# A gated product on 8192 x 8192 floats: four-row groups packed into three 64 KiB slots, with all transfers issued from one software queue

## The chip, the cores and the metric

The kernel runs on one core of a Trainium2 chip. Times are device microseconds (us). Most executions of one kernel agree within 0.3%. Every experiment below was therefore timed in five rounds beside the kernel before (nine runs of it in each batch; r0_after has four timed runs, the others five). All runs were fast, with a granted clock of 1.0.

A ratio is the mean time of one kernel's fast runs over that of the kernel before in the same rounds, so it is not quite the ratio of the medians that are quoted beside it. Brackets after it are its 95% interval.

## The reference

```python
def reference(x):                       # x: 8192 x 8192 float32
    a, b = np.split(x, 2, axis=-1)
    return a * (1 / (1 + np.exp(-b)))   # 8192 x 4096 float32
```

268.4 MB are read and 134.2 MB written. Each element needs one sigmoid (ACT, the scalar engine) and one product (DVE, the vector engine).

## The kernel before

The default path takes two rows per partition (PAIR = 2). Loads are issued from the SP queue, stores from the ACT queue.

```python
x_t   = x.rearrange("(n p r) m -> n p (r m)", p=P, r=PAIR)     # 32 tiles, 64 KiB per partition
out_t = out.rearrange("(n p r) m -> n p (r m)", p=P, r=PAIR)
for i in range(n_tiles):
    x_sb = pool.tile([P, in_cols], fp32)        # two buffers of 64 KiB
    o_sb = pool.tile([P, out_cols], fp32)       # two buffers of 32 KiB
    eng(LOAD_ENG, i).dma_start(out=x_sb, in_=x_t[i])            # SP
    n_chunks = TAIL_CHUNKS if i >= n_tiles - TAIL_ITERS else 1  # last tile in 4 chunks a row
    for r in range(PAIR):
        # ... a_part, b_part, o_part: slices of the row, n_chunks of them
        nc.scalar.activation(out=b_part, in_=b_part, func=SIG)
        nc.vector.tensor_mul(out=o_part, in0=a_part, in1=b_part)
        # ... in the last tile: store o_part at once (512 KB)
    if n_chunks == 1:
        eng(STORE_ENG, i + 1).dma_start(out=out_t[i], in_=o_sb) # ACT, 4 MiB
```

Of the kernel before, what the change touches and what calls it, by code (L numbers as in the profile page):

```python
# [2 lines left out]

# [4 lines left out]


@with_exitstack  # L10
def kernel(
    ctx: ExitStack,
    tc: tile.TileContext,
    x: bass.AP,
    out: bass.AP,
):
    nc = tc.nc
    P = nc.NUM_PARTITIONS

    PAIR = int(os.environ.get("GLU_PAIR", "2"))  # L20
    BUFS = int(os.environ.get("GLU_BUFS", "2" if PAIR == 2 else "5"))
    STORE_ENG = os.environ.get("GLU_STORE", "scalar")
    LOAD_ENG = os.environ.get("GLU_LOAD", "sync")
    TAIL_CHUNKS = int(os.environ.get("GLU_TAIL_CHUNKS", "4"))
    TAIL_ITERS = int(os.environ.get("GLU_TAIL_ITERS", "1"))

    n_rows, n_cols = x.shape
    half = n_cols // 2
    assert out.shape == (n_rows, half)

    fp32 = mybir.dt.float32
    SIG = mybir.ActivationFunctionType.Sigmoid

    def eng(name, i):
        if name == "alt":
            name = "sync" if (i % 2 == 0) else "scalar"
        return getattr(nc, name)

    pool = ctx.enter_context(tc.tile_pool(name="io", bufs=BUFS))

    if PAIR == 1:
        x_t = x.rearrange("(n p) m -> n p m", p=P)
        out_t = out.rearrange("(n p) m -> n p m", p=P)
        n_tiles = x_t.shape[0]

        for i in range(n_tiles):
            x_sb = pool.tile([P, n_cols], fp32)
            eng(LOAD_ENG, i).dma_start(out=x_sb, in_=x_t[i])

            n_chunks = TAIL_CHUNKS if i >= n_tiles - TAIL_ITERS else 1  # L50
            csz = half // n_chunks
            for c in range(n_chunks):
                lo = c * csz
                hi = lo + csz
                a_part = x_sb[:, lo:hi]
                b_part = x_sb[:, half + lo : half + hi]
                nc.scalar.activation(out=b_part, in_=b_part, func=SIG)
                nc.vector.tensor_mul(out=a_part, in0=a_part, in1=b_part)
                eng(STORE_ENG, i + 1).dma_start(out=out_t[i, :, lo:hi], in_=a_part)
    else:  # L60
        x_t = x.rearrange("(n p r) m -> n p (r m)", p=P, r=PAIR)
        out_t = out.rearrange("(n p r) m -> n p (r m)", p=P, r=PAIR)
        n_tiles = x_t.shape[0]
        in_cols = PAIR * n_cols
        out_cols = PAIR * half

        for i in range(n_tiles):
            x_sb = pool.tile([P, in_cols], fp32)
            o_sb = pool.tile([P, out_cols], fp32)
            eng(LOAD_ENG, i).dma_start(out=x_sb, in_=x_t[i])  # L70

            n_chunks = TAIL_CHUNKS if i >= n_tiles - TAIL_ITERS else 1
            for r in range(PAIR):
                a_all = x_sb[:, r * n_cols : r * n_cols + half]
                b_all = x_sb[:, r * n_cols + half : (r + 1) * n_cols]
                o_all = o_sb[:, r * half : (r + 1) * half]
                csz = half // n_chunks
                for c in range(n_chunks):
                    lo = c * csz
                    hi = lo + csz  # L80
                    a_part = a_all[:, lo:hi]
                    b_part = b_all[:, lo:hi]
                    o_part = o_all[:, lo:hi]
                    nc.scalar.activation(out=b_part, in_=b_part, func=SIG)  # L84
                    nc.vector.tensor_mul(out=o_part, in0=a_part, in1=b_part)  # L85
                    if n_chunks > 1:
                        eng(STORE_ENG, i + 1).dma_start(  # L87
                            out=out_t[i, :, r * half + lo : r * half + hi], in_=o_part
                        )
            if n_chunks == 1:  # L90
                eng(STORE_ENG, i + 1).dma_start(out=out_t[i], in_=o_sb)


# [1 line left out]
_INS = ['x']  # L95
_OUTS = [((8192, 4096), 'float32')]


# [23 lines left out]
```

## Time and profile before

The median was 937.13 us (936.40 to 937.37, three runs). The first fence holds lines of the profile page of the kernel before: busy time of each engine, DVE's and the DMA engines' busy tenths in 40 slices, what the DMA engines moved in each slice, the two DMA queues (packets, MB, share of the 16 engines' span), and the chain of waits by engine.

```profile
...
DVE 280.9 (30%) x70; ACT 230.0 (25%) x71; POOL 0.2 (0%) x4
...
DVE  0333321333213332133321333312333123331234
...
DMA  9999999999999999999999999999999999999998
GB/s 404 404 449 427 427 449 427 427 434 464 404 441 434 428 449 425 451 408 462 410 429 446 425 450 420 453 408 453 421 429 446 424 452 429 441 411 450 424 449 359
...
q1 hardware_dynamic: 4608, 268.44, 66.5%
q10 hardware_dynamic: 5616, 134.22, 33.3%
...
HBM read 268.44 MB, written 134.22 MB: 431 GB/s over the span
...
DMA 78%; DVE 15%; ACT 6%; issue 0%; DVEq 0%; ACTq 0%; SPq 0%
...
```

The two queues take 66.5% + 33.3% = 99.8% of the 16 DMA engines' time. DVE and ACT are busy for less than a third. DVE is part of the chain (15%) only because a tile's second half of work stands between a landing and the next load; while it runs, the other buffers' transfers are moving.

The trace also holds one record for each packet (one piece of a transfer, moved by one of the 16 engines), which the views above only add up. From these records:

| packet | count | usual time of one | sum / 16 engines |
|---|---|---|---|
| load, 64 KiB | 4096 | 2418 ns | 619 us |
| store, 32 KiB | 3968 | 1213 ns | 301 us |
| store of the last tile, 4 KiB | 1024 | 159 ns | 10 us |

The sum is 930 us of a span of 934.1. 65,536 bytes in 2418 ns on 16 engines are 433.7 GB/s. The Trainium skill (DMA: Bandwidth & Descriptors, Where 436 GB/s comes from) puts the ceiling of the 16 ports at 435.2 GB/s; the trace agrees. So no rearrangement can gain much more than the 4 us that are not packets.

The next fence is the timeline of the kernel before near its end: start, length, engine, line, operation, and in brackets the idle time before it with what ended it.

```profile
...
885.91 7.12 ACT L84 ACTIVATE x_sb<-x_sb 128x4096 f32<-128x4096 f32 x2 [21.92 <-DMA x_sb<-in_x_dram]
889.56 8.76 DVE L85 TENSOR_TENSOR o_sb<-x_sb 128x4096 f32<-128x4096 f32 x2 [20.28 <-ACT x_sb L84]
898.35 0.34 ACTq L91 DMA_DIRECT2D out_dram<-o_sb  x1
914.83 2.95 ACT L84 ACTIVATE x_sb<-x_sb 128x1024 f32<-128x1024 f32 x3 [21.79 <-DMA x_sb<-in_x_dram]
...
```

A tile's work starts every 28.9 us (885.91, 914.83). That is close to eight rounds of one load packet and one store packet, 8 x (2418 + 1213) = 29,048 ns: the two queues alternate, nearly packet by packet.

### The profile page before, as it was taken

The page shows a single profiled execution, that of the slowest core. Times are in us where ns is not written, and L with a number is a line of the kernel's source. Part 1 is how long each engine was busy: PE and PEld are TensorE (multiplying, and loading weights), DVE is VectorE, ACT ScalarE, POOL GpSimd, SP SyncE. Part 2 cuts the span into 40 slices and gives each one's busy share as a digit, 9 for nine tenths or more (in the row PEclk, how much of TensorE's full clock was granted, in tenths as well). Part 3 has the DMA queues.
Part 4 walks back from the last instruction along what each step waited for, and adds up shares of the span by engine and source line. Part 5 has one row for each costly group of instructions (what it writes and reads, how often), then busy time and mean ns, then how long its engine had stood idle before and what let it go on. Part 6 is the DMA issues. An engine that isn't in the chain of part 4 may idle for free.

```text
span 934.1 us, 410 instructions
## 1 busy us (share of the span) xinstructions
DVE 280.9 (30%) x70; ACT 230.0 (25%) x71; POOL 0.2 (0%) x4
## 2 busy tenths in 40 slices
DVE  0333321333213332133321333312333123331234
ACT  0313331133311333113332033320233202333023
POOL 0000000000000000000000000000000000000000
DMA  9999999999999999999999999999999999999998
GB/s 404 404 449 427 427 449 427 427 434 464 404 441 434 428 449 425 451 408 462 410 429 446 425 450 420 453 408 453 421 429 446 424 452 429 441 411 450 424 449 359
DMA packets 10226, 402.67 MB, mean 431 GB/s; under 512 B 1136, under 2 KB 1136, under 8 KB 2160
## 3 DMA queue, kind: packets, MB, share of 16 engines
q1 hardware_dynamic: 4608, 268.44, 66.5%
q10 hardware_dynamic: 5616, 134.22, 33.3%
q14 instruction: 2, 0.02, 0.0%
HBM read 268.44 MB, written 134.22 MB: 431 GB/s over the span
## 4 chain that ended last, share of the span: by engine, by line
DMA 78%; DVE 15%; ACT 6%; issue 0%; DVEq 0%; ACTq 0%; SPq 0%
DMA x_sb<-in_x_dram 78%; DVE o_sb L85 15%; ACT x_sb L84 6%; DVEq L117 0%; ACTq L87 0%; SPq L70 0%; ACTq L84 0%
## 5 line engine op out<-in xcount | busy, mean ns | idle before, releaser
L85 DVE TENSOR_TENSOR o_sb<-x_sb 128x4096 f32<-128x4096 f32 (+1 forms) x70 | 280.9, 4056 | 647.3 <-ACT x_sb L84 647.3
L84 ACT ACTIVATE x_sb<-x_sb 128x4096 f32<-128x4096 f32 (+1 forms) x70 | 228.7, 3315 | 696.1 <-DMA x_sb<-in_x_dram 692.0
L84 ACT ACT_TABLE_LOAD x1 | 1.3, 1283 | 0.7 <-PEq L106 0.7
L106 POOL MEMSET const-bfloat16-1.0<- 128x1 bf16 x1 | 0.1, 102 | 0.0
L106 POOL MEMSET const-uint8-127<- 128x1 uint8 x1 | 0.1, 102 | 0.0
L106 POOL MEMSET const-float32-1.0<- 128x1 f32 x1 | 0.1, 99 | 0.0
L106 POOL MEMSET const-float32-0.0<- 128x1 f32 x1 | 0.1, 98 | 0.2 <-issue 0.2
## 6 DMA issues: line engine op xcount, KB each, us to landing
out_dram<-o_sb ACTq DMA_DIRECT2D x31, 4096.0 KB, 41.8
out_dram<-o_sb ACTq DMA_DIRECT2D x8, 512.0 KB, 6.3
x_sb<-in_x_dram SPq DMA_DIRECT2D x32, 45.5
```

The lines of the kernel that those rows point to most:

```text
L84: nc.scalar.activation(out=b_part, in_=b_part, func=SIG)
L85: nc.vector.tensor_mul(out=o_part, in0=a_part, in1=b_part)
L106: nc = _bacc.Bacc("TRN2", target_bir_lowering=False, num_devices=1)
```

## The change

The intent, as the code shows it: 64 KiB runs in both directions, all transfers 8 MiB, no output buffers (results are packed into the slot whose inputs are already used up), and one queue whose fixed order decides which transfer comes next. The tail order (last second-half load before the last store but one) is there so that the last compute runs under a store.

```diff
-    pool = ctx.enter_context(tc.tile_pool(name="io", bufs=BUFS))
... (the old loop, shown above, goes)
+    R = 4
+    n_groups = n_rows // (P * R)
+    x_g = x.rearrange("(n p h r) m -> n h p (r m)", p=P, h=2, r=R // 2)
+    out_g = out.rearrange("(n p r) m -> n p (r m)", p=P, r=R)
+    width = 2 * n_cols
+    pool = ctx.enter_context(tc.tile_pool(name="slots", bufs=1))
+    heads = [pool.tile([P, width], fp32, name=f"head{k}") for k in range(2)]
+    tail = pool.tile([P, width], fp32, name="tail")
+    def load(g, h):
+        nc.gpsimd.dma_start(out=heads[g % 2] if h == 0 else tail, in_=x_g[g, h])
+    def compute(g):
+        head = heads[g % 2]
+        for r in range(R):
+            src = head if r < 2 else tail
+            lo = (r % 2) * n_cols
+            a = src[:, lo : lo + half]
+            b = src[:, lo + half : lo + n_cols]
+            nc.scalar.activation(out=b, in_=b, func=SIG)
+            nc.vector.tensor_mul(out=head[:, r * half : (r + 1) * half], in0=a, in1=b)
+    def store(g):
+        nc.gpsimd.dma_start(out=out_g[g], in_=heads[g % 2])
+    load(0, 0)
+    load(0, 1)
+    for g in range(n_groups):
+        last_pair = g >= n_groups - 2
+        if g + 1 < n_groups:
+            load(g + 1, 0)
+        compute(g)
+        if g + 1 < n_groups and last_pair:
+            load(g + 1, 1)
+        store(g)
+        if g + 1 < n_groups and not last_pair:
+            load(g + 1, 1)
```

The queue thus carries: load, load, load, store 0, load, load, store 1, and so on, with the last two stores side by side.

More of the change, by code (lines that the diff above doesn't have):

```diff
@@ L1 @@
-import os
 from contextlib import ExitStack
@@ L5 @@
 import concourse.tile as tile
-from concourse import bass_utils, mybir
+from concourse import mybir
 from concourse._compat import with_exitstack
@@ L18 @@
     P = nc.NUM_PARTITIONS
-    PAIR = int(os.environ.get("GLU_PAIR", "2"))
-    BUFS = int(os.environ.get("GLU_BUFS", "2" if PAIR == 2 else "5"))
-    STORE_ENG = os.environ.get("GLU_STORE", "scalar")
-    LOAD_ENG = os.environ.get("GLU_LOAD", "sync")
-    TAIL_CHUNKS = int(os.environ.get("GLU_TAIL_CHUNKS", "4"))
-    TAIL_ITERS = int(os.environ.get("GLU_TAIL_ITERS", "1"))
+    fp32 = mybir.dt.float32
+    SIG = mybir.ActivationFunctionType.Sigmoid
     n_rows, n_cols = x.shape
     half = n_cols // 2
-    assert out.shape == (n_rows, half)
@@ L31 @@
-    fp32 = mybir.dt.float32
-    SIG = mybir.ActivationFunctionType.Sigmoid
-    def eng(name, i):
-        if name == "alt":
-            name = "sync" if (i % 2 == 0) else "scalar"
-        return getattr(nc, name)
-    pool = ctx.enter_context(tc.tile_pool(name="io", bufs=BUFS))
-    if PAIR == 1:
-        x_t = x.rearrange("(n p) m -> n p m", p=P)
-        out_t = out.rearrange("(n p) m -> n p m", p=P)
-        n_tiles = x_t.shape[0]
-        for i in range(n_tiles):
-            x_sb = pool.tile([P, n_cols], fp32)
-            eng(LOAD_ENG, i).dma_start(out=x_sb, in_=x_t[i])
-            n_chunks = TAIL_CHUNKS if i >= n_tiles - TAIL_ITERS else 1
-            csz = half // n_chunks
-            for c in range(n_chunks):
-                lo = c * csz
-                hi = lo + csz
-                a_part = x_sb[:, lo:hi]
-                b_part = x_sb[:, half + lo : half + hi]
-                nc.scalar.activation(out=b_part, in_=b_part, func=SIG)
-                nc.vector.tensor_mul(out=a_part, in0=a_part, in1=b_part)
-                eng(STORE_ENG, i + 1).dma_start(out=out_t[i, :, lo:hi], in_=a_part)
-    else:
-        x_t = x.rearrange("(n p r) m -> n p (r m)", p=P, r=PAIR)
-        out_t = out.rearrange("(n p r) m -> n p (r m)", p=P, r=PAIR)
-        n_tiles = x_t.shape[0]
-        in_cols = PAIR * n_cols
-        out_cols = PAIR * half
-        for i in range(n_tiles):
-            x_sb = pool.tile([P, in_cols], fp32)
-            o_sb = pool.tile([P, out_cols], fp32)
-            eng(LOAD_ENG, i).dma_start(out=x_sb, in_=x_t[i])
-            n_chunks = TAIL_CHUNKS if i >= n_tiles - TAIL_ITERS else 1
-            for r in range(PAIR):
-                a_all = x_sb[:, r * n_cols : r * n_cols + half]
-                b_all = x_sb[:, r * n_cols + half : (r + 1) * n_cols]
-                o_all = o_sb[:, r * half : (r + 1) * half]
-                csz = half // n_chunks
-                for c in range(n_chunks):
-                    lo = c * csz
-                    hi = lo + csz
-                    a_part = a_all[:, lo:hi]
-                    b_part = b_all[:, lo:hi]
-                    o_part = o_all[:, lo:hi]
-                    nc.scalar.activation(out=b_part, in_=b_part, func=SIG)
-                    nc.vector.tensor_mul(out=o_part, in0=a_part, in1=b_part)
-                    if n_chunks > 1:
-                        eng(STORE_ENG, i + 1).dma_start(
-                            out=out_t[i, :, r * half + lo : r * half + hi], in_=o_part
-                        )
-            if n_chunks == 1:
-                eng(STORE_ENG, i + 1).dma_start(out=out_t[i], in_=o_sb)
```

## The prediction

> **What bounds it now.** The DMA engines. The page's slice table shows DMA at 9 tenths in 39 of 40 slices, mean 431 GB/s; DVE is busy 30%, ACT 25%. The queue table adds up to 99.8% (66.5% loads, 33.3% stores). In the trace's transfer records nearly every 64 KiB load packet takes 2418 ns and every 32 KiB store packet 1213 ns, alone or mixed with the other direction: about 433 GB/s on 16 engines, whatever the mix. Floor: 4096 load packets / 16 x 2.418 + 3968 store packets / 16 x 1.213 + 1024 small store packets / 16 x 0.159 = 619 + 301 + 10 = 930 us of a 934.1 us span. Only some 4 us are anything else: about 2 us before the first packet, under 1 us of slow first packets, a 1 us hiccup at the first store, and about 2 us at the end, where the 512 KB stores leave engines partly idle (windows view: DMA share 0.69 in the last 6 us). The chain of waits names loads (78%), DVE (15%) and ACT (6%), but its compute hides behind other transfers.
>
> **What the change does.** Bytes stay at 402.65 MB. Stores become 64 KiB runs: 2048 packets at an estimated 2.418 us for 3968 of 1.213 and 1024 of 0.159: about 1.5 us saved. 71 transfers become 48 of 8 MiB. Loads and stores follow each other in one queue instead of alternating by packet; with equal rates both ways that alone changes nothing.
>
> **Does the queue run dry?** From the trace: 8 MiB takes 8 x 2.418 = 19.3 us. A store needs its group's second half landed plus 3.6 (ACT) + 2 x 4.39 (DVE) = 12.4 us; meanwhile the next group's first half moves (19.3 us), which leaves 7 us to issue. The load that needs a store's completion waits while a second-half load (19.3 us) moves. At the end the last second half is loaded before the last store but one, so the last 12.4 us of compute hide too. No bubble; the final store runs at full rate: 1 to 2 us saved.
>
> **What it adds.** GpSimd writes descriptors in software. The Trainium skill (DMA: Bandwidth & Descriptors, Latency and other measured facts) gives a first byte of about 1 us against 0.6: only the first load exposes it. It also warns (SBUF — State Buffer, "DVE blocks DMA" box) that DVE 2-port operations starve this path; here issues come after the multiplies or with 7 to 19 us of slack. No run shows either yet.
>
> **Sum.** 934.1 - 1.5 (packets) - 1.5 (tail) + 0.5 (first issue) + up to 3 (direction switches in one queue) = 932 to 935 span; measured time lies 3 us above the span. I predict 936 us, range 930 to 948. Faster by over 2%: 0.01; within 2%: 0.94; slower by over 2%: 0.05.
>
> **What would show it.** One software queue, DMA at 9 throughout, about 432 GB/s; 64 KiB packets of 2.42 us both ways; each issue several us before the preceding transfer ends; unchanged ACT and DVE means (3.6, 4.4 us); no drop of DMA share in the tail.
>
> **What would make it wrong.** Descriptors cut small (4 KiB packets take 159 ns here, 5% slower per byte); one slow engine, which a serial queue cannot hide; a 1 us stall at each of the 29 direction switches, as at the first store here (3%); the 128 KiB pitch of the loads slowing HBM; descriptor generation held up by DVE beyond 7 us.

## The result

The changed kernel took 942.70 us median (940.58 to 942.86, four runs) against 936.92 (four runs): ratio 1.0059 [1.0045, 1.0073]. It is slower by 0.6%, inside the predicted range, but on the other side of the old time than the sum in the prediction. In a later batch on one chip it took 944.11 (ratio 1.0081 [1.0067, 1.0095]). The result is correct.

These are the lines of the page after that answer to those before; the last three are groups of GpSimd's DMA instructions (busy time, mean ns of one, idle before, what ended most of it).

```profile
...
DVE 281.8 (30%) x64; ACT 229.2 (24%) x65; POOL 25.7 (3%) x52
...
DVE  0452330513305133051331503315033250332430
...
DMA  9999999999999999999999999999999999999997
GB/s 401 432 415 443 404 446 446 426 421 446 426 421 443 446 415 432 446 426 432 435 440 429 429 437 435 429 432 432 443 424 432 440 443 412 437 443 412 437 415 315
...
q0 software_dynamic: 6912, 402.66, 99.2%
...
HBM read 268.44 MB, written 134.22 MB: 428 GB/s over the span
...
issue 79%; DMA 14%; POOL 2%; DVE 1%; ACT 0%; POOLq 0%; PEldq 0%; ACTq 0%
...
L53 POOL DMA_DIRECT2D out_dram<-head x16 | 8.6, 536 | 496.6 <-DVE head L50 496.6
L40 POOL DMA_DIRECT2D head<-in_x_dram x16 | 8.6, 536 | 358.8 <-DMA out_dram<-head 358.0
L40 POOL DMA_DIRECT2D tail<-in_x_dram x16 | 8.4, 527 | 31.6 <-DVE head L50 31.3
...
```

DVE and ACT do the same work in the same time. One software queue carries all. DMA stays at 9 until the last slice, where it is 7 and moves 315 GB/s, before 359. GpSimd needs 527 to 536 ns for one issue. The chain of waits is of no use for this kernel: 79% of it is "issue", time in which the profile shows nothing that the engine waited for.

The windows view shows the end more closely. Columns: window, its length, busy time of DVE, ACT and POOL with instruction counts, clock, DMA share, GB/s. First the kernel before, where the DMA share drops at 930:

```profile
...
core 0: us, DVE busy (x) ACT busy (x) POOL busy (x), PEclk, DMA share, GB/s
...
700.00:800.00 100.00, 26.28 (x6) 22.53 (x7) 0.00 (x0) 1.00 1.01 436
...
925.00:930.00 5.00, 2.36 (x2) 1.83 (x2) 0.00 (x0) 1.00 1.03 420
930.00:935.00 5.00, 0.00 (x0) 0.00 (x0) 0.00 (x0) 1.00 0.41 169
935.00:942.00 7.00, 0.00 (x0) 0.00 (x0) 0.00 (x0) 1.00 0.00 0
...
```

Then the changed kernel, with the same windows:

```profile
...
700.00:800.00 100.00, 26.46 (x6) 21.37 (x6) 2.11 (x4) 1.00 1.00 433
...
925.00:930.00 5.00, 0.00 (x0) 0.00 (x0) 0.00 (x0) 1.00 1.00 433
930.00:935.00 5.00, 0.00 (x0) 0.00 (x0) 0.00 (x0) 1.00 0.64 275
935.00:942.00 7.00, 0.00 (x0) 0.00 (x0) 0.00 (x0) 1.00 0.02 9
...
```

In the middle (700 to 800) nothing is lost: share 1.00 and 433 GB/s. Three things are to be seen at the end. There is a drop after 930 here too. It is slow: a share of 0.64 for 5 us means that some engines are done and others are not; 0.02 of 7 us on 16 engines is 2.2 us, about one packet of one engine. And the span ends at 941 us, some 3 us after that last packet.

The packet records give the whole account, in us. "Slow" is what packets took beyond 2418, 1213 or 159 ns, averaged over the 16 engines; "last engine" is how much later the last engine ends than the mean of all; "after" is the time from the last byte to the end. In these tables the end, and with it the span, is the start of the last instruction, 0.05 us before the end of the span on the page. The columns add up to some 1 to 1.5 us more than the span, because successive packets' records overlap by 3 to 4 ns; the kernel before has more packets, so the differences add up to 6.2 and not to 6.8.

| | first packet starts | packets, usual length | slow | last engine | after | span |
|---|---|---|---|---|---|---|
| before | 1.73 | 930.0 | 1.81 | 0.7 | 1.30 | 934.1 |
| after | 2.65 | 928.5 | 4.91 | 2.7 | 3.02 | 940.9 |
| difference | +0.9 | -1.5 | +3.1 | +2.0 | +1.7 | +6.8 |

Three of these differences need no argument. The packets became fewer and cheaper, as foreseen (-1.5). The first packet starts 1.38 us after GpSimd's issue begins, before 1.00 us after SP's; the Trainium skill's difference of 0.4 us (1 against 0.6, DMA: Bandwidth & Descriptors, Latency and other measured facts) agrees, and another 0.54 us pass because GpSimd begins its first issue at 1.27 us and SP at 0.73. At the end, GpSimd has a DRAIN instruction on record that ends 2.0 us after SP has seen the last store land; in the kernel before, GpSimd's drain at the end is over long before.

The slow packets are not spread out; they gather where one transfer follows another. The records do not name the engine, but joining each to the one that ends where it starts gives 16 chains. In the changed kernel 167 packets after the first 70 us are over 30 ns slow. Of these 114 are the last packet of a load that is followed by a store (2.1 of 3.2 us), 27 stand at a change from a store to a load (0.4 us; that load had been issued some 20 us before, 815.86 for packets that start from 833.6 on), and 15 are the first packet of the very last load (0.4 us). At the first store, all 16 engines are slow, by 0.8 to 1.2 us; at the second 13 by up to 0.35 us; later between 3 and 15 by up to 1 us. The kernel before has one such place, also at its first store, and then practically none (0.10 us from 70 us on, against 3.30). The engines that are hit fall behind: at the end, 11 of the 16 finish within 0.4 us of each other, the other five 1.4 to 3.4 us after the median.

### The profile page after: what moved, and what is told of

The parts are those of the page before. It is cut to its first block, busy times and chain, and to the rows that moved or that the text cites. A ratio compares the mean times of both kernels' runs of the same rounds, so it can differ in the third digit from the quotient of the medians.

```text
span 941.0 us, 315 instructions
## 1 busy us (share of the span) xinstructions
DVE 281.8 (30%) x64; ACT 229.2 (24%) x65; POOL 25.7 (3%) x52
## 4 chain that ended last, share of the span: by engine, by line
issue 79%; DMA 14%; POOL 2%; DVE 1%; ACT 0%; POOLq 0%; PEldq 0%; ACTq 0%
DMA head<-in_x_dram 6%; DMA tail<-in_x_dram 5%; DMA out_dram<-head 3%; DVE head L50 1%; POOL out_dram L53 1%; POOL head L40 1%; POOL tail L40 1%; ACT tail L49 0%; POOLq L92 0%; POOLq L53 0%; POOLq L40 0%; PEldq L92 0%; ACTq L49 0%
## 5 line engine op out<-in xcount | busy, mean ns | idle before, releaser
L50 DVE TENSOR_TENSOR head<-tail 128x4096 f32<-128x4096 f32 x32 | 140.2, 4422 | 438.1 <-ACT tail L49 438.1
L49 ACT ACTIVATE tail<-tail 128x4096 f32<-128x4096 f32 x32 | 114.0, 3608 | 467.4 <-DMA tail<-in_x_dram 467.4
L50 DVE TENSOR_TENSOR head<-head 128x4096 f32<-128x4096 f32 x32 | 141.6, 4425 | 192.2 <-ACT head L49 190.5
L49 ACT ACTIVATE head<-head 128x4096 f32<-128x4096 f32 x32 | 114.0, 3608 | 209.4 <-DMA head<-in_x_dram 209.4
L53 POOL DMA_DIRECT2D out_dram<-head x16 | 8.6, 536 | 496.6 <-DVE head L50 496.6
L40 POOL DMA_DIRECT2D head<-in_x_dram x16 | 8.6, 536 | 358.8 <-DMA out_dram<-head 358.0
L40 POOL DMA_DIRECT2D tail<-in_x_dram x16 | 8.4, 527 | 31.6 <-DVE head L50 31.3
```

The source lines that it names most:

```text
L40: nc.gpsimd.dma_start(out=heads[g % 2] if h == 0 else tail, in_=x_g[g, h])
L49: nc.scalar.activation(out=b, in_=b, func=SIG)
L50: nc.vector.tensor_mul(out=head[:, r * half : (r + 1) * half], in0=a, in1=b)
L53: nc.gpsimd.dma_start(out=out_g[g], in_=heads[g % 2])
```

## The experiments

Candidate explanations for the slow packets and the lagging engines were:

- A: the software path (descriptors written by GpSimd) makes packets slow.
- B: one serial queue that alternates loads and stores makes them slow at each load-to-store switch.
- C: the successor of the slow packet was issued too late.

The table holds all twelve experiments in the columns of the table above (one profiled execution each), with medians and ratios of five rounds. The first four ran on one chip, so did the next four and the last four, on three different chips. Kernels are best compared by their ratios to the kernel before: the changed kernel itself took 942.70 us in one batch and 944.11 in another.

| run | us, median | ratio to before | first | packets | slow | last engine | after | span |
|---|---|---|---|---|---|---|---|---|
| r0_after | 944.11 | 1.0081 [1.0067, 1.0095] | 2.64 | 928.5 | 7.34 | 3.0 | 3.02 | 944.0 |
| e1_sp | 939.75 | 1.0035 [1.0023, 1.0048] | 1.74 | 928.5 | 4.85 | 2.5 | 1.13 | 937.8 |
| e2_two | 981.09 | 1.0477 [1.0455, 1.0499] | 1.72 | 928.5 | 26.50 | 0.1 | 1.12 | 977.0 |
| e3_last_sp | 943.43 | 1.0067 [1.0054, 1.0081] | 2.62 | 928.5 | 6.26 | 2.7 | 1.16 | 940.4 |
| e4_short | 938.24 | 1.0018 [1.0004, 1.0032] | 1.73 | 928.5 | 3.19 | 2.1 | 1.23 | 935.7 |
| d1_sp | 938.42 | 1.0022 [1.0009, 1.0034] | 1.72 | 928.5 | 3.26 | 2.8 | 1.19 | 936.6 |
| b1_loads_pool | 937.41 | 1.0008 [0.9996, 1.0021] | 2.60 | 930.0 | 2.16 | 0.9 | 1.23 | 935.7 |
| b2_stores_pool | 937.41 | 1.0010 [0.9997, 1.0022] | 1.75 | 930.0 | 1.97 | 0.5 | 2.82 | 935.5 |
| d2_pool | 943.62 | 1.0073 [1.0059, 1.0087] | 2.62 | 928.5 | 4.51 | 4.8 | 2.99 | 942.4 |
| d3_grouped | 934.12 | 0.9974 [0.9961, 0.9986] | 1.74 | 928.5 | 1.53 | 0.4 | 1.10 | 932.3 |
| d4_half | 941.12 | 1.0048 [1.0035, 1.0060] | 1.73 | 929.5 | 3.15 | 5.0 | 1.10 | 939.1 |
| e5_pool_short | 941.30 | 1.0049 [1.0037, 1.0062] | 2.64 | 928.5 | 3.27 | 2.4 | 3.08 | 938.9 |

The kernel before had medians of 936.95, 936.66 and 936.71 us.

### r0_after: the changed kernel again

> The changed kernel again, as the yardstick of this call. Every theory expects 941 to 943 us, ratio to the kernel before about 1.006, a software queue, slow packets (over 2418 ns) mostly at the last load packet before each store, and the last engine finishing some 3 us after the first.

It took 944.11 us, above the expected range by 1 us. The extra time is in the slow packets (7.34 us against 4.91 in the first profile); first packet and end are alike to 0.01 us. The slow packets are thus the part that differed most between these two executions; whether by run or by chip is not known. Their places differ too: of 221, some 90 are the last packet of a load before a store and some 80 stand at a change from a store to a load, where together they cost 1.6 us. The kernel is not edited.

### e1_sp: every transfer from the SP queue

```diff
-        nc.gpsimd.dma_start(out=heads[g % 2] if h == 0 else tail, in_=x_g[g, h])
+        nc.sync.dma_start(out=heads[g % 2] if h == 0 else tail, in_=x_g[g, h])
-        nc.gpsimd.dma_start(out=out_g[g], in_=heads[g % 2])
+        nc.sync.dma_start(out=out_g[g], in_=heads[g % 2])
```

> The changed kernel with every transfer issued from the SP queue instead of GpSimd; order, slots, waits and bytes are the same. Theory A (the software path costs the 5.8 us: 0.9 us later first packet, 2 us GpSimd drain at the end, and 3 to 5 us of slow packets and engine skew): 935 to 937 us, no slow packets but the first few. Theory B (the single serial queue makes the slow packets and the skew at each direction switch, the software path only the first packet and the drain): 939 to 940.5 us, slow packets still at each load-to-store switch.

939.75 us, as B has it: 4.4 us less than with GpSimd, and still 2.8 us more than the kernel before. Of the 4.4, the first packet gives 0.9 and the end 1.9; the slow packets stay (170 packets over 30 ns slow after the first 70 us, 167 and 221 in the two profiles with GpSimd). 132 of the 170 are the last packet of a load before a store, and those at a change from a store to a load, 16, cost 0.2 us. Theory A alone falls: slow packets and lagging engines are there without any software descriptor.

### e2_two: the new slots with loads on SP and stores on ACT

```diff
-        nc.gpsimd.dma_start(out=heads[g % 2] if h == 0 else tail, in_=x_g[g, h])
+        nc.sync.dma_start(out=heads[g % 2] if h == 0 else tail, in_=x_g[g, h])
-        nc.gpsimd.dma_start(out=out_g[g], in_=heads[g % 2])
+        nc.scalar.dma_start(out=out_g[g], in_=heads[g % 2])
```

> The changed kernel with loads from the SP queue and stores from the ACT queue, same three slots. If alternating queues only share the engines, as the trace of before shows, a store and the second-half load beside it end together after about 39 us, and the load that waits for that store starts only after it has landed: a bubble of about 2 us in each of 14 groups, 955 to 965 us. If the single queue is itself a cost (theory B) and no bubble arises: 934 to 937 us.

It is slower than both expectations, 981.09 us. Two queues are no improvement in themselves; the three slots need the fixed order. The timeline near the end shows why:

```profile
...
895.88 0.36 ACTq L53 DMA_DIRECT2D out_dram<-head  x1
...
943.02 7.12 ACT L49 ACTIVATE tail<-tail 128x4096 f32<-128x4096 f32 x2 [26.69 <-DMA tail<-in_x_dram]
946.67 8.76 DVE L50 TENSOR_TENSOR head<-tail 128x4096 f32<-128x4096 f32 x2 [24.86 <-ACT tail L49]
955.46 0.34 ACTq L53 DMA_DIRECT2D out_dram<-head  x1
```

The store of group 14 is issued at 895.88 us and shares the engines with the second-half load of group 15, and the load lands at 943 us. Then the last sigmoid and the last product run with almost nothing left to move, and the last store is issued at 955.46. The windows view of the same run (columns as above):

```profile
...
820.00:880.00 60.00, 17.61 (x4) 14.25 (x4) 0.00 (x0) 1.00 0.99 418
...
941.00:957.00 16.00, 8.76 (x2) 7.12 (x2) 0.00 (x0) 1.00 0.15 66
957.00:977.00 20.00, 0.00 (x0) 0.00 (x0) 0.00 (x0) 1.00 0.85 367
...
```

From 941 to 957 the DMA share is 0.15: about 14 us are lost there, which my expectation had left out. Most of the rest are slow packets: 24.7 us of them after the first 70 us, nearly all of them load packets, about 1 to 1.7 us in most groups just before a store joins and mostly 0.4 to 0.9 us around its end. So slow packets come in two queues as well, where the store queue runs empty in each group. The bubbles that I expected between groups come to about 5 us of gaps in the records. So the fixed order in one queue is worth a lot with these slots; it does not follow that it is better than the order before with its own buffers.

### e3_last_sp: only the last store from SP

```diff
-        nc.gpsimd.dma_start(out=out_g[g], in_=heads[g % 2])
+        q = nc.sync if g == n_groups - 1 else nc.gpsimd
+        q.dma_start(out=out_g[g], in_=heads[g % 2])
```

> The changed kernel with only the last store moved to the SP queue. If the 2 us GpSimd drain after the last transfer is charged to software transfers still in flight, it ends earlier and 1.5 to 2 us are saved: 940.5 to 941 us. The last two stores then share the engines packet by packet, which costs nothing. If the drain is charged to the queue as such: 942 to 943 us.

The first theory is the one that says that software transfers still in flight hold the drain up. The end of the span behaves as it says: GpSimd's drain ends at 927 us, under the last store, and the time after the last byte falls from 3.02 to 1.16 us. The total hardly shows it: 943.43 against 944.11, with overlapping intervals and above both expected ranges, so the gain in time is inconclusive; the slow packets, which vary by more than that, were not touched.

### e4_short: on SP, compute cut to 256 columns

The two edits of e1_sp, and this one:

```diff
-            nc.scalar.activation(out=b, in_=b, func=SIG)
-            nc.vector.tensor_mul(out=head[:, r * half : (r + 1) * half], in0=a, in1=b)
+            nc.scalar.activation(out=b[:, :256], in_=b[:, :256], func=SIG)
+            nc.vector.tensor_mul(out=head[:, r * half : r * half + 256], in0=a[:, :256], in1=b[:, :256])
```

> The SP version of the changed kernel (939.75 us) with the sigmoid and the product done on 256 of 4096 columns only; wrong result on purpose. Order, slots, waits and bytes are unchanged, but each store is issued some 18 us before the engines need it, not 5. Theory C (a packet is slow because its successor's descriptors came late): the slow packets before stores vanish, apart from the first few, and 936 to 937 us. Theory B (one serial queue pays at every load-to-store switch): the slow packets stay, 939 to 940 us.

Its output is wrong, which doesn't matter for the time. 938.24 us lies between the theories. Slow packets become fewer (107 after 70 us, from 170) and cost 1.49 us there, from 3.09, but they do not vanish. Theory C is at most a part. The ratio's interval overlaps a little with that of e1_sp, and the cut takes away both the lateness and the work of ACT and DVE beside the transfers, so this run does not tell those two apart.

### d1_sp: transfers alone, same order, on SP

```diff
-    ... (heads, tail, compute and the loop)
+    src = pool.tile([P, width], fp32, name="src")
+    ring = [pool.tile([P, width], fp32, name=f"ring{k}") for k in range(2)]
+    nc.sync.dma_start(out=src, in_=x_g[0, 0])
+    nc.sync.dma_start(out=ring[0], in_=x_g[0, 1])
+    nc.sync.dma_start(out=ring[1], in_=x_g[1, 0])
+    nc.sync.dma_start(out=out_g[0], in_=src)
+    for k in range(3, 2 * n_groups):
+        nc.sync.dma_start(out=ring[(k - 1) % 2], in_=x_g[k // 2, k % 2])
+        if k % 2 == 0:
+            nc.sync.dma_start(out=out_g[k // 2 - 1], in_=src)
+    nc.sync.dma_start(out=out_g[n_groups - 1], in_=src)
```

> Transfers alone on the SP queue in the same load-load-store order: all stores read one slot that was loaded once, loads alternate between two slots, no compute; wrong result on purpose. Everything is issued 38 us or more ahead. Theory C: 934 to 936 us and no slow packets after the first few. Theory B: 938 to 940 us and slow packets at each switch. If e4_short keeps its slow packets and this one has none, the coupling through landings (a load issued only when a store has landed on the slowest engine) is the cause.

Its output is wrong, which doesn't matter for the time. 938.42 us, in the range of B, with slow packets at the switches: all 16 at the first, 15 and 16 at the second and third, then fewer. There is no compute here, no load waits for a store, and nothing is issued late: a load waits for the landing of the load before it in its slot, but that still leaves some 38 us. So late issue, compute and loads that wait for stores are not needed for slow packets: the order in the queue is enough.

### b1_loads_pool and b2_stores_pool: the software path in the kernel before

```diff
-    LOAD_ENG = os.environ.get("GLU_LOAD", "sync")        # b1
+    LOAD_ENG = os.environ.get("GLU_LOAD", "gpsimd")
-    STORE_ENG = os.environ.get("GLU_STORE", "scalar")    # b2, alone
+    STORE_ENG = os.environ.get("GLU_STORE", "gpsimd")
```

> The kernel before with its loads issued from GpSimd instead of SP; two queues as before. If the software path costs only its later first packet (0.9 us) where its transfers are done before the end: 937.5 to 938.5 us. If software descriptors slow the packets themselves: 940 us or more, with slow packets all along.

> The kernel before with its stores issued from GpSimd instead of ACT. If the software path costs only the GpSimd drain after the last store (1.9 us): 938.5 to 939.5 us. If software descriptors slow the packets themselves: 941 us or more.

Both took 937.41 us, 0.75 us more than the kernel before; the intervals of both ratios include 1. The profiles show where the fixed costs sit: with loads from GpSimd the first packet starts at 2.60 us, with stores from GpSimd the time after the last byte is 2.82 us. Each run has three packets over 30 ns slow after the first 70 us. Software descriptors thus do not make packets slow where loads and stores sit in two queues. b2's time was below its expected range: the span of its profile, 935.5 us, is 1.4 us above that of the first profile of the kernel before, and the timed runs show half of that.

### d2_pool: d1_sp from GpSimd

```diff
-    nc.sync.dma_start(out=src, in_=x_g[0, 0])
+    nc.gpsimd.dma_start(out=src, in_=x_g[0, 0])
... (and so for every transfer)
```

> d1_sp (transfers alone, everything issued early, 938.4 us) with every transfer from GpSimd. If the software path costs only its first packet (0.9 us) and the drain (1.9 us): 941 to 941.7 us, slow packets as in d1_sp. If software descriptors add slow packets in a single queue even when issued early: 942.5 us or more.

943.62 us, above both: 5.2 us over d1_sp, or 4.8 us by the ratios, since the two ran on different chips. The two fixed costs make 2.7 us of it. In the two profiles the rest is slow packets (+1.3) and the lag of the last engine (+2.0). So in one alternating queue the software path seems to add to what B describes, even with everything issued early; with one profile of each, on different chips, this is not settled. Why it should do so only there, no run shows.

### d3_grouped: all loads, then all stores

```diff
-    nc.sync.dma_start(out=out_g[0], in_=src)
     for k in range(3, 2 * n_groups):
         nc.sync.dma_start(out=ring[(k - 1) % 2], in_=x_g[k // 2, k % 2])
-        if k % 2 == 0:
-            nc.sync.dma_start(out=out_g[k // 2 - 1], in_=src)
-    nc.sync.dma_start(out=out_g[n_groups - 1], in_=src)
+    for g in range(n_groups):
+        nc.sync.dma_start(out=out_g[g], in_=src)
```

> d1_sp with all 32 loads first and then all 16 stores: one load-to-store switch in place of 15. Theory B (each switch in one queue costs a little, and not alike on all engines): 935.5 to 937 us, slow packets only at the start and at the one switch, all engines ending within 1.5 us. If the switches are not the cause: 938 to 939 us and the engines end 4 us apart, as in d1_sp.

934.12 us: the same packets in the same queue as d1_sp, in another order, take 4.3 us less (4.5 us by the ratios; the two ran on different chips), and not one packet after the first 70 us is more than 30 ns slow. In the two profiles 1.7 us of it are slow packets and 2.4 us the lag of the last engine. The end of both in the windows view (no DVE or ACT instructions, so the columns are window, length, POOL, clock, DMA share, GB/s), first d1_sp, then d3_grouped:

```profile
...
700.00:800.00 100.00, 0.00 (x0) 1.00 1.00 431
...
925.00:930.00 5.00, 0.00 (x0) 1.00 1.03 446
930.00:935.00 5.00, 0.00 (x0) 1.00 0.18 79
...
```

```profile
...
700.00:800.00 100.00, 0.00 (x0) 1.00 0.99 430
...
925.00:930.00 5.00, 0.00 (x0) 1.00 0.97 419
930.00:935.00 5.00, 0.00 (x0) 1.00 0.00 0
...
```

d3_grouped has no packet that starts after 930 us; its engines end between 930.6 and 931.2. In d1_sp the last engine ends at 935.4, 3.6 us after the median one. This is the decisive pair. The next run, d4_half, alternates on SP too and ran on the chip of d3_grouped in the same rounds: it took 7.0 us more, of which only 1.0 us is the usual length of its packets. One detail goes against my wording of B: even the one switch from load to store (at 621 us) shows no slow packet. What costs is a store that begins between loads, in a queue that goes back to loading.

d3_grouped is no rival for a real kernel: it computes nothing, and a kernel cannot hold all loads before the first store.

### d4_half: stores cut in two, twice as many switches

The loop starts at k = 2 here and runs two steps past the last load.

```diff
-        if k % 2 == 0:
-            nc.sync.dma_start(out=out_g[k // 2 - 1], in_=src)
+        g, h = divmod(k - 2, 2)
+        cols = slice(h * n_cols, (h + 1) * n_cols)
+        nc.sync.dma_start(out=out_g[g][:, cols], in_=src[:, cols])
```

> d1_sp with each store cut in two halves of 4 MiB (32 KiB runs), one after each load: 31 load-to-store switches in place of 15. The 32 KiB packets add 1.0 us by their nominal length (2 x 1213 against 2418 ns, 2048 pairs on 16 engines). Theory B: 941 us or more, twice as many places with slow packets. If the switches are not the cause: 939 to 940 us.

941.12 us, as B has it, 2.7 us above d1_sp, of which 1.0 us is the usual length of the smaller packets. There are 30 switches (the expectation counts 31) and about twice as many places with slow packets as in d1_sp, but their sum is the same as in d1_sp (3.15 against 3.26 us). Fewer engines are hit at each switch (mostly one to five). What grew is the lag of the last engine, 5.0 us from 2.8, and the kernel ends with that one. The cost is therefore not a fixed price for each switch.

### e5_pool_short: the changed kernel with short compute

The edit is that of e4_short, with all transfers left on GpSimd.

> The changed kernel, all on GpSimd, with the compute cut to 256 of 4096 columns; wrong result on purpose. Stores are issued some 18 us ahead. If the late issue of stores and loads is what the software path aggravates: 940.5 to 941.5 us (e4_short, 938.24, plus 0.9 and 1.9), that is 2 to 3 us less than the changed kernel. If not: 943 to 944 us.

Its output is wrong, which doesn't matter for the time. 941.30 us, as the first theory (late issue is what the software path makes worse) has it: 2.8 us less than r0_after, with intervals that do not overlap, and 3.1 us more than e4_short, which the two fixed costs (0.9 and 1.85 us) nearly make up. But it is only 1.4 us less than the first batch of the changed kernel, whose interval does overlap, so the gain in time is not firm. The packets say more: 93 are slow after 70 us, for 1.4 us in all, against 167 and 221, and the 27 and 80 at a change from a store to a load are down to 3. So with short compute the software path seems to cost its fixed part only, in this kernel; d2_pool, issued early too, paid more. How a short lead comes about is seen in the timeline of the changed kernel. The start:

```profile
...
42.79 7.12 ACT L49 ACTIVATE tail<-tail 128x4096 f32<-128x4096 f32 x2 [12.20 <-DMA tail<-in_x_dram]
46.44 8.76 DVE L50 TENSOR_TENSOR head<-tail 128x4096 f32<-128x4096 f32 x2 [10.37 <-ACT tail L49]
55.49 0.54 POOL L53 DMA_DIRECT2D out_dram<-head  x1 [52.51 <-DVE head L50]
56.02 0.53 POOL L40 DMA_DIRECT2D tail<-in_x_dram  x1
63.03 7.12 ACT L49 ACTIVATE head<-head 128x4096 f32<-128x4096 f32 x2 [13.12 <-DMA head<-in_x_dram]
66.68 8.95 DVE L50 TENSOR_TENSOR head<-head 128x4096 f32<-128x4096 f32 x2 [11.49 <-ACT head L49]
83.00 0.53 POOL L40 DMA_DIRECT2D head<-in_x_dram  x1 [26.45 <-DMA out_dram<-head]
...
```

The store is issued at 55.49, and the load before it lands at 63.03, so there are about 7 us of lead. Near the end:

```profile
...
860.63 7.12 ACT L49 ACTIVATE tail<-tail 128x4096 f32<-128x4096 f32 x2 [31.59 <-DMA tail<-in_x_dram]
864.28 8.76 DVE L50 TENSOR_TENSOR head<-tail 128x4096 f32<-128x4096 f32 x2 [29.75 <-ACT tail L49]
873.33 0.53 POOL L40 DMA_DIRECT2D tail<-in_x_dram  x1 [31.27 <-DVE head L50]
873.85 0.54 POOL L53 DMA_DIRECT2D out_dram<-head  x1
880.09 7.12 ACT L49 ACTIVATE head<-head 128x4096 f32<-128x4096 f32 x2 [12.34 <-DMA head<-in_x_dram]
...
```

The second-half load of group 15 is issued at 873.33, when the last product of group 14 is done (864.28 + 8.76, plus waits). The load ahead of it lands at 880.09, so 7 us seem to be left as before. But a landing is that of the last engine. By the packet records, the ten fastest engines had finished that load at 875.3 to 875.6 us and the last one at 879.7. For the fast ones the lead was 2 us, and their packets just there were up to 1.0 us slow (summed over all 16 engines and divided by 16, 0.5 us; 0.69 us in r0_after; 0.02 in e1_sp, which had the same lead of 2 us but whose queue issues a transfer in 0.33 us). Lateness is thus a follow-up cost of the lag, seen with the software queue only; that it is lateness and not the missing compute that makes e5_pool_short faster is not shown. It cannot explain the slow packets at the end of stores, since the load that follows had been issued some 20 us ahead.

## Why the prediction was right or wrong

The time fell into the range (930 to 948) and within 2%, both as predicted. The centre, 936, missed by 6.7 us, and the change of 0.6% to the slower side was not foreseen. The range held because it was wide on the slow side, not because the sum was right: the sum has a span of 932 to 935 us, and it was 941.0. Its largest error is the tail, -1.5 us in the sum and +3.7 us in the profile. A smaller one is the step from span to time, 3 us in the sum and about 2 us in the runs. Point by point:

- **"What bounds it now: the DMA engines"** was right. Share 1.00 in the middle of both kernels; usual packet length 930.0 and 928.5 us.
- **"About 1.5 us saved" by 64 KiB stores** was right: 1.5 us. Their packets take 2418 ns, as estimated.
- **"Does the queue run dry?"** No bubble was right: the DMA share in mid-kernel is 1.00. The lead of 7 us was right for the last engine and wrong for the others, since I treated 16 engines as one. Engines that had pulled ahead had 2 us at the end.
- **"The final store runs at full rate: 1 to 2 us saved"** is a step that failed, and with it "no drop of DMA share in the tail". The tail lost instead: the last engine ends 2.7 us after the mean (before 0.7), and GpSimd's drain adds 1.7 us after the last byte. e3_last_sp shows that the drain belongs to software transfers in flight. I had no term for it.
- **"Only the first load exposes it"** (the software path) was right about the start, in size a little low (+0.9 us against +0.5), and overlooked the end. That software descriptors do not slow packets held in two queues (b1, b2), not fully in one (d2_pool).
- **"Up to 3 us for direction switches"** was a term of the sum that was mis-sized. Slow packets cost 3.1 us more than before in the first profile (5.5 in the second), plus 2.0 us of lag. I had seen the one slow place in the kernel before and had put "a 1 us stall at each of the 29 direction switches" among the risks. d1_sp and d3_grouped show that alternation in one queue costs 4.3 us; but it is not 1 us at each switch, and in the changed kernel some of it stands at changes from a store to a load too (0.4 and 1.6 us in the two profiles). Why those places are slow there and hardly in e1_sp, d2_pool and e5_pool_short, no run shows.
- **"With equal rates both ways that alone changes nothing"** is the sentence behind that term, and it failed. Equal rates of single packets do not make orders of packets equal.
- Of the risks, "one slow engine, which a serial queue cannot hide" came in another form: five of 16 engines ended 1.4 to 3.4 us after the median. Small descriptors did not come (64 KiB packets throughout), and a slowing by the 128 KiB pitch of the loads did not either (2418 ns). A stall of descriptors behind DVE was never on trial: in the two profiles of the changed kernel no issue ran beside a product, so the skill's warning (SBUF — State Buffer, "DVE blocks DMA" box) is neither confirmed nor refuted here.

What stays open is the mechanism: why a load packet takes up to 1.2 us longer when a store begins between loads in one queue, why d3_grouped's single switch escapes, why e2_two has slow packets in two queues, and why some engines are hit more often. The trace does not name the engine of a packet, so whether it is always the same ones cannot be read.

## What to carry to other kernels

Add up the packets' usual times before changing a transfer-bound kernel: here they left 4 us of 934, so a reordering could lose more than it could win. Two queues that always both have work let loads and stores alternate at no visible cost, while the same alternation in 8 MiB pieces in one queue set the 16 engines apart, and every landing and the end of the kernel follow the last engine. If a software queue must be used, let it not carry the last transfer (1.9 us at the end of the profile of e3_last_sp, though the timed runs do not show the gain), and count the lead of an issue from the first engine that needs it.

## What the Trainium skill lacked or had wrong

- DMA: Bandwidth & Descriptors, Issuing engines are not separate DMA queues, says that transfers from all issuing engines run on the same 16 DMA engines and interleave. The trace of the kernel before agrees (its two queues alternate, and a tile starts every 28.9 us). The page does not say that order within one queue matters: the same transfers took 938.42 us alternating and 934.12 us grouped (d1_sp, d3_grouped).
- The same page, Latency and other measured facts, calls DMA engines 7 and 15 usually slower and guesses at the software descriptor rings as the cause, "SWDGE-specific". Which engines lag cannot be read here, but in d1_sp, on a hardware queue alone, the last engine ended 3.6 us after the median one; software rings cannot be the only cause of lagging engines, if these are the engines that the page means. With GpSimd the last one ended 6.6 us after the median (d2_pool).
- No page has the drain at the end of a program whose last transfers come from GpSimd: 2.8 to 3.1 us from the last byte to the end of the span, against 1.1 to 1.3 where the last transfers come from a hardware queue.
- The first-byte difference of 0.4 us on that page was confirmed (1.38 against 1.00 us from the start of the issue to the first packet; each is 0.4 us above the page's own figure, 1 and 0.6). Its ceiling of 435.2 GB/s was met within 0.4% (433.7) in a program on one core.
